# A hybrid mixer block on one core: gates, branch outputs and merge token-major with 512-column moving weights, paired scan heads, new lane paces

## The chip, the cores and the metric

The kernel runs on one core of one Trainium2 chip. The time is device microseconds of one execution. The kernel before takes 2150.59 us, the median of three runs (2144.82 to 2153.54). One more execution was profiled; its own time is 2151.65 us and its span, from the first instruction to the last, is 2149.9 us.

## The reference, cut to what matters

One layer on 256 tokens of width 2048, with a second sequence of 256 context tokens that only feeds the scans' start states. All data is float32.

```python
h  = rms_norm(x, norm_g[0]) * (1 + sc1) + sh1           # sc, sh, g come from c @ mod_w
u  = h @ w_in                                           # 2048 -> 14168 columns, the last 8192 are gates
u_ssd, u_rwkv, u_conv, u_fft, u_gate = split(u)
p_ssd  = ssd_branch(u_ssd)     @ ssd_out                # chunked scan, 12 heads of 64, 4 groups
p_rwkv = rwkv_branch(u_rwkv)   @ rwkv_out               # 8 heads of 64, forward and backward
p_conv = conformer_branch(u_conv) @ conv_out            # 31-tap depthwise convolution
p_fft  = fourier_branch(u_fft) @ fourier_out
gates  = sigmoid(u_gate).reshape(b, l, 4, 2048)
m = gates[:,:,0]*p_conv + gates[:,:,1]*p_ssd + gates[:,:,2]*p_fft + gates[:,:,3]*p_rwkv
y = m @ w_o
x = x + g1 * rms_norm(y, norm_g[1])
h = rms_norm(x, norm_g[2]) * (1 + sc2) + sh2
out = x + g2 * rms_norm(square(relu(h @ mlp_up)) @ mlp_down, norm_g[3])
```

In the scan, each head of 128-token chunks is `(C B^T * L) xd` inside the chunk plus `C state * exp(a)`; the two directions are summed, multiplied by `silu(z)` and normed over all 768 channels before `ssd_out`. The context is scanned for its states alone.

## The kernel before, in words

Each large product is done with three float32r products: a weight and an activation are both split into a rounded part `hi` and a rest `lo`, and hi·hi, hi·lo and lo·hi are summed in PSUM (`mm3`, lines 178 to 180). A **unit** is two k-tiles of 128 rows by 512 weight columns, 512 KB. SyncE fetches it into `raw` (line 155, three buffers), ScalarE rounds it to `hi` (line 166), VectorE subtracts to get `lo` (line 167), five buffers of 512 columns each. `block` makes a product feature-major: the weight is the stationary operand of a matmul, 128 columns at a time, and 256 tokens are streamed past it, 24 matmuls of 256 columns for a unit. `rowblock` makes it token-major: 128 tokens of the activation are stationary and 512 weight columns are streamed, 12 matmuls of 512 columns. Before the change `rowblock` serves the Fourier input, `w_o` and `mlp_down`; `block` serves everything else.

The order of the work: start-up (norms, modulation, first input columns, to about 200 us), the other input columns, 16 **gate blocks** of 8 units each (`mid2`, 640 to 1206 us), the four **branch outputs** (`outs`, in the order rwkv, fft, conv, ssd; 36 units, to about 1300 us), `w_o`, and the two halves of the MLP (from 1405 us to the end). A gate block goes through tanh into a buffer `gs` and to DRAM (`g_d`), and `outs` reads it back as `gt`, computes `(gt + 1) * acc` on VectorE and adds it to the merged `m`; `m` is split into the stationary tiles `hx` of `w_o`.

Beside this **foreground** run **lanes**: generators for the RWKV scan, the 31 taps, the chunked scan (`ssd`, line 1256 on), Fourier and conformer, and a lane that multiplies `mod_w` on VectorE (`rm` loads, line 1448; `macc`, line 1455). After every unit `step` gives each lane a budget of 2.4 times its rate, and the lane issues code until that is used up; a lane's instructions carry a priority offset (`ROFF`, `SOFF`, `COFF`, `TOFF`) by which the scheduler may put them ahead of earlier foreground code. The scheduler fixes the order on each engine when the program is built; every engine then works through its list strictly in that order. A branch output whose lane isn't done first drains that lane (`while n not in self.f_done: self.step(4.0)`).

The chunked scan starts when the RWKV scan has passed a point in its last quarter: `side_setup` loads constants, then for each of 4 groups a 5-tap convolution (`conv5`, lines 1247 to 1253), `C B^T` (1344), states (1364), and for each of 3 heads a table of decays (GpSimd 1374, ScalarE 1378 to 1388), two products (VectorE 1389 to 1399) and four matmuls (1407, 1409) of 64 output rows into half of a PSUM bank. Each second head closes a pair (VectorE 1416, 1419). When all six pairs are there, `chnorm` norms them (1220 to 1232) and they are split for `ssd_out`.

Of the kernel before, what the change touches and what calls it, by code (L numbers as in the profile page):

```python
# [9 lines left out]
ALU = mybir.AluOpType  # L10
P = 128
OFFS = 100
RATE_RWKV = 1.4
RATE_SIDE = .508
RATE_CONV = .279
AHEAD = 2
S2 = 11
ROFF = 100
SOFF = 100
S1 = 14  # L20
WT = dict(a=1.0, A=.813, b=.999, c=.72)
MR = .26, .26, .109, .244
HB = 5
B4 = 8
COFF = -100
MB = 3
XB = 8
MW = 6
RATE_TAPS = .183
TOFF = -200  # L30
GR = 1, 1, 2, 2, 2, 4, 4
RAWB = 3
# [61 lines left out]
class K:  # L94
# [493 lines left out]
    def mid2(self, prep, er, open_ssd, open_side):  # L588
# [18 lines left out]
        cols(C_VAL, self.evac_val)  # L607
        self.lane(self.taps(), rate=RATE_TAPS, offs=TOFF)
# [3 lines left out]
        cols(C_Z + 512, lambda i, ps: self.spill(self.cz_d[4], ps), 2)  # L612
        ssd = side = False
        for b in range(16):
            cols(C_G + 512 * b, gate(b))
            if not ssd and {("A", 3), ("b", 3), ("c", 2)} <= self.rw_done:

                ssd = True
                for st in prep:
                    st.close()  # L620
                self.sd = open_ssd()
                self.side_setup()
                self.lane(self.ssd(), rate=RATE_SIDE, offs=SOFF)
            if not side and not self.rwl["gens"]:
                side = True
                er.close()
                self.fc = open_side()
                self.lane(self.fft(), self.conv(), rate=RATE_CONV, offs=COFF)
# [627 lines left out]
    def ssd(self):  # L1256
# [66 lines left out]
        py = None  # L1323
        for hf in range(2):
            xtk = self.S("b6", [P, 4, 384])
            for f in range(3):
# [9 lines left out]
            for gl in range(2):  # L1336
# [30 lines left out]
                for hl in range(3):  # L1367
# [28 lines left out]
                    for d in range(2):  # L1396
# [2 lines left out]
                        nc.vector.scalar_tensor_tensor(Ce[:, d, l2], row[:, 1 - d, d], et[:, 2 + d, hd[d]:hd[d] + 1],  # L1399
                                                       Cc[:, l2], op0=ALU.mult, op1=ALU.mult)  # L1400
                    yield 2.5
                    if h % 2 == 0:
# [106 lines left out]
    def outs(self, op):  # L1509
# [3 lines left out]
        for n in ("rwkv", "fft", "conv", "ssd"):  # L1513
# [12 lines left out]
                F = [(F[0][:, i], F[1][:, i]) for i in range(k)]  # L1526
            for b in range(4):
                gt = [self.t(op, "gt", [P, 512], bufs=4) for _ in range(2)]
                for i in range(2):
                    nc.sync.dma_start(gt[i], self.g_d[(gi * 16 + b * 4) // 2 + i])  # L1530
                acc = [self.t(self.pa, "acc", [P, 512]) for _ in range(2)]
                for u in range(k // 2):
                    wu = self.unit([(self.wap(io[wname][0], 2 * u, 2, 512 * b, 512), 0)], 2, 512)
                    for f in range(4):
                        for i in range(2):
# [12 lines left out]
                for i in range(2):  # L1548
                    m, om = half(self.m[b], i), half(old, i)
                    if first:  # L1550
                        nc.vector.scalar_tensor_tensor(m, gt[i], 1.0, acc[i], op0=ALU.add, op1=ALU.mult)
                    else:
                        nc.vector.scalar_tensor_tensor(gt[i], gt[i], 1.0, acc[i], op0=ALU.add, op1=ALU.mult)
                        (nc.vector if n == "ssd" else nc.gpsimd).tensor_tensor(m, om, gt[i], op=ALU.add)
# [188 lines left out]
```

## Time and profile before

| | |
|---|---|
| median of three runs | 2150.59 us |
| profiled execution, its own time | 2151.65 us |
| its span | 2149.9 us |
| TensorE matmuls busy | 2058.0 us, 96% |
| VectorE busy | 1503.0 us, 70% |
| ScalarE busy | 1022.7 us, 48% |
| GpSimd busy | 251.9 us, 12% |
| mean granted TensorE clock | 0.990 |

How to read it: matmuls overlap one another, so an interval between two starts, not a duration, is what a matmul costs; a stretch that is 100% busy divided by its count gives that. The profile counts an instruction in the stretch it touches. A float32 matmul without the hand-made split is recorded twice.

### The profile page before, as it was taken

Reading aid. Unit: us, or ns where it says so; the run is one execution under the profiler, and the core shown is the slowest. Engines: PE = TensorE matmul, PEld = TensorE weight load, DVE = VectorE, ACT = ScalarE, POOL = GpSimd, SP = SyncE. Lnnn points to the kernel's source line nnn. Section 1 sums busy time; section 2 is a strip of 40 time slices with the busy share of each in tenths; the row PEclk is TensorE's granted clock in tenths of the full one; section 3 lists DMA queues with packets and bytes.
Section 4 is the critical chain, followed back from the end, with each engine's and each line's share of the span. In section 5 each row is a group of like instructions: output and inputs, shape, how many; then the busy total and the mean of one; then the engine's idle time right before and its main releaser. Section 6 shows DMA issues by size and latency. Waiting matters only on the chain.

```text
span 2149.9 us, 39741 instructions
## 1 busy us (share of the span) xinstructions
PE 2058.0 (96%) x14894; PEld 1884.8 (88%) x14894; DVE 1503.0 (70%) x2699; ACT 1022.7 (48%) x1934; POOL 251.9 (12%) x285
## 2 busy tenths in 40 slices
PE   6999999999999999899999999999999999999997
PEld 5758999998989999798888998899998889999886
DVE  5645875679999779587987787565766655555555
ACT  4212443454654554355666645464554444545443
POOL 1001430022131022021221140000000000000001
PEclk9999999999999999899999999999999999999999
DMA  9983636767666765579876677546867666666554
GB/s 337 318 273 106 186 87 203 234 165 219 197 187 201 214 185 167 177 219 299 265 247 197 205 270 263 188 124 184 262 205 271 234 210 185 185 185 192 192 194 157
DMA packets 310828, 450.99 MB, mean 210 GB/s; under 512 B 70969, under 2 KB 116700, under 8 KB 310124
## 3 DMA queue, kind: packets, MB, share of 16 engines
q1 hardware_dynamic: 308716, 441.86, 65.9%
q10 hardware_dynamic: 1472, 6.49, 0.9%
q8 instruction: 117, 1.92, 0.4%
q14 instruction: 75, 0.61, 0.1%
q0 software_dynamic: 448, 0.11, 0.0%
HBM read 424.22 MB, written 24.16 MB: 209 GB/s over the span
## 4 chain that ended last, share of the span: by engine, by line
PE 71%; DVE 11%; DMA 10%; issue 3%; SPq 2%; ACT 1%; POOL 1%; DVEq 0%; ACTq 0%; POOLq 0%
PE acc L180 20%; PE acc L179 20%; PE acc L178 20%; DMA rm<-in_mod_w 3%; DVE lo L167 2%; DMA raw<-in_w_in 2%; PE sm L282 2%; DVE macc L1455 2%; PE sm L1009 1%; DMA t<-scrA 1%; ACT hi L166 1%; DMA scrA<-x 1%; DMA raw<-in_fourier_out 1%; DVE tm L800 1%; SPq L278 1%
## 5 line engine op out<-in xcount | busy, mean ns | idle before, releaser
L167 DVE TENSOR_TENSOR lo<-raw,hi 128x512 fp32r<-128x512 f32 x1096 | 760.8, 712 | 434.4 <-ACT hi L166 414.6
L166 ACT CAST hi<-raw 128x512 fp32r<-128x512 f32 x1096 | 651.6, 617 | 800.0 <-PE acc L179 442.6
L180 PE MATMUL acc<-h,lo 128*128 128x256 f32 x3056 | 861.6, 286 | 16.1 <-DVE lo L167 15.8
L178 PE MATMUL acc<-h,hi 128*128 128x256 f32 x3056 | 865.7, 286 | 7.7 <-ACT hi L166 5.0
L179 PE MATMUL acc<-h,hi 128*128 128x256 f32 x3056 | 864.7, 285 | 1.5 <-DVE h L173 1.5
L180 PEld LDWEIGHTS acc<-h,lo 128*128 128x128 f32 x3056 | 575.2, 190 | 31.0 <-DVE lo L167 21.4
L178 PEld LDWEIGHTS acc<-h,hi 128*128 128x128 f32 x3056 | 578.4, 190 | 27.0 <-issue 11.8
L179 PEld LDWEIGHTS acc<-h,hi 128*128 128x128 f32 x3056 | 580.0, 190 | 16.4 <-issue 13.4
L1455 DVE SCALAR_TENSOR_TENSOR macc<-rm,sct,macc 128x512 f32<-128x512 f32 x240 | 193.1, 805 | 68.4 <-DMA rm<-in_mod_w 66.9
L179 PE MATMUL acc<-lo,uh 128*128 128x512 f32 x512 | 200.1, 391 | 0.0
L180 PE MATMUL acc<-hi,ul 128*128 128x512 f32 x512 | 199.3, 389 | 0.0
L178 PE MATMUL acc<-hi,uh 128*128 128x512 f32 x512 | 179.0, 389 | 0.0
L178 PEld LDWEIGHTS acc<-hi,uh 128*128 128x128 f32 x512 | 96.1, 188 | 19.9
L179 PEld LDWEIGHTS acc<-lo,uh 128*128 128x128 f32 x512 | 96.1, 188 | 19.9 <-DVE lo L167 0.2
L180 PEld LDWEIGHTS acc<-hi,ul 128*128 128x128 f32 x512 | 96.1, 188 | 19.8
L1689 POOL TENSOR_TENSOR yg<-yg,grow 128x512 f32<-128x512 f32 x8 | 10.9, 1368 | 721.5 <-ACT junk L1688 721.5
L179 PE MATMUL acc<-lo,h 128*128 128x512 f32 x160 | 63.9, 399 | 1.6 <-DVE lo L167 1.6
L180 PE MATMUL acc<-hi,h 128*128 128x512 f32 x160 | 63.3, 396 | 0.0
L1180 DVE SCALAR_TENSOR_TENSOR cv<-vp,col,cv 128x256 f32<-128x256 f32 x120 | 62.7, 523 | 0.4
L472 DVE TENSOR_TENSOR ua<-acc,ua 128x512 f32<-128x512 f32 (+1 forms) x50 | 34.0, 687 | 38.9 <-PE acc L180 38.6
L178 PE MATMUL acc<-hi,h 128*128 128x512 f32 x160 | 57.5, 396 | 1.1 <-ACT hi L166 1.1
L282 PE MATMUL sm<-mw,s 128*32 128x256 f32 (+2 forms) x448 | 57.0, 450 | 0.0
(379 smaller groups left out, 2476.7 us busy)
## 6 DMA issues: line engine op xcount, KB each, us to landing
raw<-in_w_in SPq DMA_DIRECT2D x216, 512.0 KB, 4.5
rm<-in_mod_w SPq DMA_DIRECT2D x256, 256.0 KB, 3.6
raw<-in_mlp_up SPq DMA_DIRECT2D x128, 512.0 KB, 3.6
raw<-in_mlp_down SPq DMA_DIRECT2D x128, 512.0 KB, 4.0
mw<-in_mod_w SPq DMA_DIRECT2D x64, 512.0 KB, 6.1
raw<-in_w_o SPq DMA_DIRECT2D x32, 512.0 KB, 3.6
gd<-gs SPq DMA_DIRECT2D x32, 256.0 KB, 4.3
gt<-gd SPq DMA_DIRECT2D x32, 256.0 KB, 3.4
```

Source lines behind the costliest of these rows:

```text
L166: nc.scalar.copy(b, a)
L167: nc.vector.tensor_tensor(c, a, b.bitcast(F32), op=ALU.subtract)
L178: nc.tensor.matmul(out, w[0], x[0], start=st, stop=False, skip_group_check=True)
L179: nc.tensor.matmul(out, w[0], x[1], start=False, stop=False, skip_group_check=True)
L180: nc.tensor.matmul(out, w[1], x[0], start=False, stop=sp, skip_group_check=True)
L278: nc.sync.dma_start(raw, self.wap(self.io["mod_w"][0], k, ke, c0, w))
L282: nc.tensor.matmul(ps[32 * j:32 * j + 32, :], self.s32[:, u + i, :], ws[i], start=u + i < 4, stop=u + i >= KT - 4, skip_group_check=True)
L472: nc.vector.tensor_tensor(ua[:m], ps[:m], ua[:m], op=ALU.add)
L800: nc.vector.tensor_tensor(o, Y[:, :r, u:u + 1].broadcast_to([P, r, n]), U[:, u:u + 1, u + 1:].broadcast_to([P, r, n]), op=ALU.mult)
L1009: nc.tensor.matmul(ch(ps, i), self.tb[n][d][:, i], ch(v, i), start=True, stop=True)
L1180: nc.vector.scalar_tensor_tensor(o, v, w, o, op0=ALU.mult, op1=ALU.add)
L1455: nc.vector.scalar_tensor_tensor(acc, raw, w, acc, op0=ALU.mult, op1=ALU.add)
```

## The change

- A gate block now goes through `rowblock`: the normed activation is stationary, 512 gate columns are streamed. The gates are stored token-major, 128 tokens by 512 columns to a tile, in as many tiles as before.
- The branch outputs go through `rowblock` in the same way, and `m` is kept token-major. Since `w_o` needs the features on the partitions, the new `mcols` transposes `m` with 32 matmuls against the identity, two PSUM banks for each 512 columns, and splits from PSUM. For 512 columns it is called one block later, for the last at the end.
- The even head of a scan pair issues no matmuls of its own; the odd head issues all eight, alternating between the halves of the bank.
- Rates, priority offsets and weights of the lanes have other values, and the RWKV lane has one buffer of tag `x2` fewer.

```diff
-RATE_RWKV = 1.4
-RATE_SIDE = .508
+RATE_RWKV = 1.451
+RATE_SIDE = 0.69
...
-SOFF = 100
+SOFF = 30
...
-RATE_TAPS = .183
+RATE_TAPS = 0.348
...
         def gate(b):
-            def evac(i, ps):
+
+            def evac(t, acc):
                 o = self.GS()
-                nc.scalar.activation(o, ps, AF.Tanh, scale=0.5)
-                nc.sync.dma_start(self.g_d[2 * b + i], o)
-            return evac
+                nc.scalar.activation(o, acc, AF.Tanh, scale=0.5)
+                nc.sync.dma_start(self.g_d[2 * b + t], o)
+            self.rowblock(win, C_G + 512 * b, range(KT), lambda kt: self.h("x", kt), evac)
...
+                    terms = [(xtk[:, 2 + i, xo:xo + 64], G[:, i]) for i in range(2)]
+                    terms += [(S0[:, d, 64 * hl:64 * hl + 64], Ce[:, d]) for d in range(2)]
                     if h % 2 == 0:
+                        even = terms
+                    else:
                         py = self.psm()
-                    o = py[64 * (h % 2):64 * (h % 2) + 64, :TOK]
-                    xo = (192 * gl + 64 * hl)
-                    for i in range(2):
-                        nc.tensor.matmul(o, xtk[:, 2 + i, xo:xo + 64], G[:, i], start=i == 0, stop=False)
-                    for d in range(2):
-                        nc.tensor.matmul(o, S0[:, d, 64 * hl:64 * hl + 64], Ce[:, d], start=False, stop=d == 1)
+                        for n in range(4):
+                            for j, (w, v) in enumerate((even[n], terms[n])):
+                                nc.tensor.matmul(py[64 * j:64 * j + 64, :TOK], w, v, start=n == 0, stop=n == 3,
+                                                 skip_group_check=True)
...
-                acc = [self.t(self.pa, "acc", [P, 512]) for _ in range(2)]
-                for u in range(k // 2):
-                    wu = self.unit([(self.wap(io[wname][0], 2 * u, 2, 512 * b, 512), 0)], 2, 512)
-                    for f in range(4):
-                        for i in range(2):
-                            kt = 2 * u + i
-                            c = (f % 2) * TOK
-                            self.mm3(acc[f // 2][:, c:c + TOK], (wu[i][0][:, f * P:f * P + P], wu[i][1][:, f * P:f * P + P]),
-                                     F[kt], u == 0 and i == 0 and f % 2 == 0,
-                                     u == k // 2 - 1 and i == 1)
-                    self.step(2.4)
...
+                self.rowblock(io[wname][0], 512 * b, range(k), lambda kt: F[kt], evac)
+                if n == "ssd":
+                    if b == 0:
+                        self.hx = ([], [])
+                    else:
+                        self.mcols(b - 1)
             first = False
-        self.hx = ([], [])
-        for b in range(4):
-            self.hsplit(self.hx, self.m[b], self.p0)
+        self.mcols(3)
+
+    def mcols(self, b):
+
+        nc = self.nc
+        m = self.m[b].rearrange("p f t -> p (f t)").rearrange("p (t c) -> p t c", t=2)
+        for i in range(0, 4, 2):
+            ps = self.psm()
+            for q in range(2):
+                for t in range(2):
+                    o = q * TOK + t * P
+                    nc.tensor.transpose(ps[:, o:o + P], m[:, t, (i + q) * P:(i + q) * P + P], self.cs("ident"))
+            self.hsplit(self.hx, ps.rearrange("p (q c) -> p q c", q=2), self.p0, i)
```

The order of instructions moves far beyond these lines, since the lanes are issued at other places. Three places follow. The line numbers of the changed kernel differ by a few; each sentence names the lines.

**TensorE, the end of the chunked scan.** Before, its last pair of heads (1407, 1409 into `sm_14824`) stands among the matmuls of the first branch output (`acc_14754`, `acc_14755`), with two more branch outputs still to come ahead of `ssd_out`:

```order
L178 MATMUL acc_14755<-f_2872_14746,hi_14796 128x256
L179 MATMUL acc_14755<-f_2873_14747,hi_14796 128x256
L1407 MATMUL sm_14824<-s_2902_14884,b_2585_13090 64x256 x2
L1409 MATMUL sm_14824<-s_2904_14893,s_2825_14487 64x256 x2
L180 MATMUL acc_14754<-f_2872_14746,lo_14797 128x256
L178 MATMUL acc_14754<-f_2872_14746,hi_14792 128x256
L179 MATMUL acc_14754<-f_2873_14747,hi_14792 128x256
L180 MATMUL acc_14754<-f_2872_14746,lo_14793 128x256
```

Now the last group's `C B^T` (1345), states (1365) and its pairs (1413) stand behind the last matmul of the third branch output (`acc_13914`), and no foreground matmul follows until the norm is done:

```order
L179 MATMUL acc_13914<-lo_13944,f_3019_13743 128x512
L180 MATMUL acc_13914<-hi_13943,f_3020_13744 128x512
L1345 MATMUL sm_12304<-s_2629_12189,s_2628_12188 128x256 x2
L1351 MATMUL sm_12309<-cst,s_2628_12188 128x128 x2
L1365 MATMUL sm_12315<-s_2660_12316,s_2657_12312 128x192 x2
L1413 MATMUL sm_12423<-s_2611_12122,b_2469_11522 64x256
L1365 MATMUL sm_12315<-s_2661_12320,s_2657_12312 128x192 x2
L1413 MATMUL sm_12423<-s_2670_12359,b_2469_11522 64x256
L1413 MATMUL sm_12423<-s_2611_12122,b_2469_11522 64x256
L1413 MATMUL sm_12423<-s_2670_12359,b_2469_11522 64x256
L1413 MATMUL sm_12423<-s_2613_12131,s_2563_11918 64x256
```

In the changed program 26 rows, 30 matmuls of the scan and its norm, stand in one piece here, and then the first matmul of `ssd_out`, whose stationary operand is the scan's result.

**VectorE, the same place.** Before, the two evacuations of a third-branch block (1553) have splits (167) for the last branch behind them:

```order
L1553 SCALAR_TENSOR_TENSOR gt_15709<-gt_15709,acc_15713 128x512
L1553 SCALAR_TENSOR_TENSOR gt_15710<-gt_15710,acc_15714 128x512
L167 TENSOR_TENSOR lo_15834<-raw_15827,hi_15833 128x512
L167 TENSOR_TENSOR lo_15864<-raw_15861,hi_15863 128x512
L167 TENSOR_TENSOR lo_15868<-raw_15861,hi_15867 128x512
L167 TENSOR_TENSOR lo_15908<-raw_15905,hi_15907 128x512
L167 TENSOR_TENSOR lo_15912<-raw_15905,hi_15911 128x512
L167 TENSOR_TENSOR lo_15942<-raw_15939,hi_15941 128x512
```

Now the evacuation of the third branch's last accumulator (1548, `acc_13914`) stands ahead of the last tap of the last group's convolution (1250), and the rest of the scan, 29 rows to the split of its result, stands behind that, ahead of the next `lo` but one:

```order
L167 TENSOR_TENSOR lo_13998<-raw_13991,hi_13997 128x512
L1548 SCALAR_TENSOR_TENSOR gt_13910<-gt_13910,acc_13914 128x512
L1250 SCALAR_TENSOR_TENSOR s_2628_12188<-pd_12190,col_9690,s_2628_12188 128x512
L167 TENSOR_TENSOR lo_14016<-raw_14013,hi_14015 128x512
L1254 TENSOR_TENSOR s_2628_12188<-s_2628_12188,s_2641_12243 128x512
L1254 TENSOR_TENSOR s_2629_12189<-s_2629_12189,s_2648_12278 128x256
L1360 TENSOR_TENSOR s_2660_12316<-b_2469_11522,s_wg 128x384
L1360 TENSOR_TENSOR s_2661_12320<-b_2469_11522,s_wg 128x384
L1391 SCALAR_TENSOR_TENSOR s_2670_12359<-s_2669_12351,s_dt,s_2655_12307 128x128 x2
L1400 SCALAR_TENSOR_TENSOR s_2672_12368<-s_2667_12347,s_et,s_2629_12189 128x128 x2
```

The scan's last group has moved from among the foreground to behind it.

**SyncE's queue, the set-up of the chunked scan.** Before, between two `raw` loads there stand 54 transfers, 14 of them `rm` loads of the modulation lane; a piece of that:

```order
L1109 DMA cst_10470<-in_cst 128x512
L239 DMA pk_10472<-in_ssd_conv_w 70x128
L1448 DMA rm_10462<-in_mod_w 128x512
L1001 DMA tb_2817<-scrD_2812 32x4x32 x2
L1001 DMA tb_2814<-scrD_2812 32x4x32 x2
L239 DMA pk_10472<-in_ssd_conv_b 14x128
L239 DMA pk_10472<-in_ssd_norm_g 6x128
L239 DMA pk_10472<-in_conv_ln_g 4x128
L239 DMA pk_10472<-in_conv_ln_b 4x128
L1448 DMA rm_10573<-in_mod_w 128x512
L1448 DMA rm_10647<-in_mod_w 128x512
L1001 DMA tb_2816<-scrA_2810 32x4x32 x2
```

Now the 54 have become one gap of 14 transfers and one of 19 with two `raw` loads between them, and no `rm` load stands in either; the end of the second:

```order
L239 DMA pk_9682<-in_ssd_conv_b 14x128
L239 DMA pk_9682<-in_ssd_norm_g 6x128
L239 DMA pk_9682<-in_conv_ln_g 4x128
L239 DMA pk_9682<-in_conv_ln_b 4x128
L1002 DMA tb_2815<-scrA_2810 32x4x32 x2
L1242 DMA pd_10267<-ssdd_2361 128x2x256
L1242 DMA pd_10096<-ssdd_2360 128x2x256
L1242 DMA pd_10341<-ssdd_2362 128x2x256
L605 DMA gd_2390<-gs_11246 128x512
L155 DMA raw_11450<-in_w_in 128x2x512
L155 DMA raw_11500<-in_w_in 128x2x512
```

The `rm` loads have moved to later gate blocks, a few between each two `raw` loads.

## Rows read from the trace of the kernel before

**Rows 1.** page of before, part 1: engine, busy us, share, instructions.

```profile
PE 2058.0 (96%) x14894; PEld 1884.8 (88%) x14894; DVE 1503.0 (70%) x2699; ACT 1022.7 (48%) x1934; POOL 251.9 (12%) x285
```

**Rows 2.** busy time of each engine by stretch; the first line names columns.

```profile
core 0: us, PE busy (x) PEld busy (x) DVE busy (x) ACT busy (x) POOL busy (x), PEclk, DMA share, GB/s
500.00:700.00 200.00, 192.09 (x1529) 183.01 (x1530) 195.53 (x422) 106.19 (x210) 36.90 (x28) 1.00 0.69 202
860.00:910.00 50.00, 41.14 (x293) 38.91 (x293) 25.20 (x47) 15.75 (x33) 0.37 (x6) 0.83 0.61 181
900.00:1210.00 310.00, 295.96 (x2255) 274.12 (x2256) 254.09 (x455) 181.19 (x382) 67.48 (x95) 1.00 0.75 237
```

**Rows 3.** the same view, in three stretches without a lane of matmuls.

```profile
1430.00:1590.00 160.00, 160.00 (x1355) 160.00 (x1354) 100.33 (x157) 79.78 (x140) 0.00 (x0) 1.00 0.70 211
1330.00:1400.00 70.00, 70.00 (x302) 56.32 (x301) 39.14 (x59) 35.19 (x64) 0.00 (x0) 1.00 0.60 196
2000.00:2050.00 50.00, 50.00 (x222) 41.39 (x221) 28.59 (x39) 23.87 (x41) 2.64 (x2) 1.00 0.57 191
```

**Rows 4.** TensorE in order of time, one scan head: start, us, line, tiles.

```profile
1204.46 1.08 PE L1407 MATMUL sm<-s,b 128*64 128x256 f32 x4
1205.38 1.03 PE L1409 MATMUL sm<-s,s 128*64 128x256 f32 x4
```

**Rows 5.** the same view in the start-up, four-column-group matmuls.

```profile
59.68 1.26 PE L282 MATMUL sm<-mw,s 128*32 128x256 f32 x20
```

**Rows 6.** the same view, a run of 128-wide matmuls.

```profile
1404.63 7.31 PE L1616 MATMUL sm<-cst 128*128 128x128 f32 x64
```

**Rows 7.** SyncE's DMA queue in order of time, when the scan is set up.

```profile
850.19 1.80 SPq L155 DMA_DIRECT2D raw<-in_w_in  x2
869.97 2.31 SPq L1448 DMA_DIRECT2D rm<-in_mod_w  x2
892.66 0.43 SPq L155 DMA_DIRECT2D raw<-in_w_in  x1
```

**Rows 8.** view of Rows 2, five of these microseconds.

```profile
885.00:890.00 5.00, 4.04 (x16) 3.56 (x16) 2.59 (x4) 1.38 (x3) 0.00 (x0) 0.50 0.87 234
```

**Rows 9.** VectorE by line and shape, 640 to 1300 us: busy, mean ns.

```profile
L167 DVE TENSOR_TENSOR lo<-raw,hi 128x512 fp32r<-128x512 f32 x315 | 226.6, 738 | 58.9 <-ACT hi L166 56.5 <-PE acc L180 1.8
L1249 DVE SCALAR_TENSOR_TENSOR s<-pd,col,s 128x512 f32<-128x512 f32 x40 | 32.6, 815 | 0.4 <-ACT s L1247 0.3
L1390 DVE SCALAR_TENSOR_TENSOR s<-s,s_dt,s 128x128 f32<-128x128 f32 x24 | 13.3, 586 | 2.0 <-ACT s L1380 1.9
L1553 DVE SCALAR_TENSOR_TENSOR gt<-gt,acc 128x512 f32<-128x512 f32 x20 | 12.9, 678 | 0.0
L1253 DVE TENSOR_TENSOR s<-s,s 128x512 f32<-128x512 f32 x10 | 7.4, 743 | 2.9 <-POOL s L658 2.9
L1232 DVE SCALAR_TENSOR_TENSOR b<-b,col,s 128x256 f32<-128x256 f32 x6 | 2.5, 478 | 0.0
L1226 DVE RECIPROCAL s<-s 128x256 f32<-128x256 f32 x1 | 1.8, 1753 | 1.1 <-ACT s L1225 1.1
```

**Rows 10.** ScalarE, the same view, 900 to 1300 us.

```profile
L1378 ACT ACTIVATE s<-s,s_nb 128x128 f32<-128x128 f32 x48 | 15.4, 392 | 6.7 <-POOL s L1374 6.6
L657 ACT ACTIVATE s<-s 128x512 f32<-128x512 f32 x10 | 6.3, 630 | 1.7 <-DVE s L1249 1.7
L1225 ACT ACT_TABLE_LOAD x2 | 2.6, 1283 | 0.0
```

**Rows 11.** GpSimd, the same view, 900 to 1300 us.

```profile
L1554 POOL TENSOR_TENSOR h<-h,gt 128x512 f32<-128x512 f32 x16 | 24.0, 1524 | 50.0 <-DVE gt L1553 50.0
L1374 POOL TENSOR_TENSOR s<-s,cst 128x512 f32<-128x512 f32 x12 | 18.3, 1526 | 94.7 <-DVE macc L1455 39.3 <-PE acc L180 33.0 <-DMA s<-crow 22.3
L1398 POOL TENSOR_TENSOR s<-s,s 128x128 f32<-128x128 f32 x24 | 14.1, 609 | 21.5 <-ACT s L1381 21.5
L658 POOL TENSOR_SCALAR s<-s 128x512 f32<-128x512 f32 x10 | 10.2, 1017 | 27.9 <-ACT s L657 27.9
```

More of the change, by code (lines that the diff above doesn't have):

```diff
@@ L12 @@
 OFFS = 100
-RATE_RWKV = 1.4
-RATE_SIDE = .508
-RATE_CONV = .279
+RATE_RWKV = 1.451
+RATE_SIDE = 0.69
+RATE_CONV = 0.28
 AHEAD = 2
 S2 = 11
-ROFF = 100
-SOFF = 100
+ROFF = 68
+SOFF = 30
 S1 = 14
-WT = dict(a=1.0, A=.813, b=.999, c=.72)
-MR = .26, .26, .109, .244
+WT = {'a': 1.0, 'A': 0.728, 'b': 1.021, 'c': 0.887}
+MR = (0.26, 0.264, 0.109, 0.244)
 HB = 5
 B4 = 8
-COFF = -100
+COFF = -295
 MB = 3
-XB = 8
+XB = 7
 MW = 6
-RATE_TAPS = .183
+RATE_TAPS = 0.348
 TOFF = -200
@@ L614, in mid2 @@
         for b in range(16):
-            cols(C_G + 512 * b, gate(b))
+            gate(b)
             if not ssd and {("A", 3), ("b", 3), ("c", 2)} <= self.rw_done:
@@ L1322, in ssd @@
         neg = self.cst2[:, 256:512].rearrange("p (o d l) -> p o d l", o=1, d=2).broadcast_to([P, 2, 2, P])
-        py = None
+        py = even = None
         for hf in range(2):
@@ L1401, in ssd @@
                     yield 2.5
+                    xo = (192 * gl + 64 * hl)
+                    terms = [(xtk[:, 2 + i, xo:xo + 64], G[:, i]) for i in range(2)]
+                    terms += [(S0[:, d, 64 * hl:64 * hl + 64], Ce[:, d]) for d in range(2)]
                     if h % 2 == 0:
+                        even = terms
+                    else:
                         py = self.psm()
-                    o = py[64 * (h % 2):64 * (h % 2) + 64, :TOK]
-                    xo = (192 * gl + 64 * hl)
-                    for i in range(2):
-                        nc.tensor.matmul(o, xtk[:, 2 + i, xo:xo + 64], G[:, i], start=i == 0, stop=False)
-                    for d in range(2):
-                        nc.tensor.matmul(o, S0[:, d, 64 * hl:64 * hl + 64], Ce[:, d], start=False, stop=d == 1)
+                        for n in range(4):
+                            for j, (w, v) in enumerate((even[n], terms[n])):
+                                nc.tensor.matmul(py[64 * j:64 * j + 64, :TOK], w, v, start=n == 0, stop=n == 3,
+                                                 skip_group_check=True)
                     yield 0.5
@@ L1528, in outs @@
                 gt = [self.t(op, "gt", [P, 512], bufs=4) for _ in range(2)]
-                for i in range(2):
-                    nc.sync.dma_start(gt[i], self.g_d[(gi * 16 + b * 4) // 2 + i])
-                acc = [self.t(self.pa, "acc", [P, 512]) for _ in range(2)]
-                for u in range(k // 2):
-                    wu = self.unit([(self.wap(io[wname][0], 2 * u, 2, 512 * b, 512), 0)], 2, 512)
-                    for f in range(4):
-                        for i in range(2):
-                            kt = 2 * u + i
-                            c = (f % 2) * TOK
-                            self.mm3(acc[f // 2][:, c:c + TOK], (wu[i][0][:, f * P:f * P + P], wu[i][1][:, f * P:f * P + P]),
-                                     F[kt], u == 0 and i == 0 and f % 2 == 0,
-                                     u == k // 2 - 1 and i == 1)
-                    self.step(2.4)
+                for t in range(2):
+                    nc.sync.dma_start(gt[t], self.g_d[2 * (4 * gi + b) + t])
                 if first:
@@ L1547, in outs, with evac @@
                     self.m[b] = self.t(op, "m", [P, 4, TOK])
-                for i in range(2):
-                    m, om = half(self.m[b], i), half(old, i)
+                def evac(t, acc):
+                    m, om = half(self.m[b], t), half(old, t)
                     if first:
-                        nc.vector.scalar_tensor_tensor(m, gt[i], 1.0, acc[i], op0=ALU.add, op1=ALU.mult)
+                        nc.vector.scalar_tensor_tensor(m, gt[t], 1.0, acc, op0=ALU.add, op1=ALU.mult)
                     else:
-                        nc.vector.scalar_tensor_tensor(gt[i], gt[i], 1.0, acc[i], op0=ALU.add, op1=ALU.mult)
-                        (nc.vector if n == "ssd" else nc.gpsimd).tensor_tensor(m, om, gt[i], op=ALU.add)
-            first = False
-        self.hx = ([], [])
-        for b in range(4):
-            self.hsplit(self.hx, self.m[b], self.p0)
+                        nc.vector.scalar_tensor_tensor(gt[t], gt[t], 1.0, acc, op0=ALU.add, op1=ALU.mult)
+                        (nc.vector if n == "ssd" else nc.gpsimd).tensor_tensor(m, om, gt[t], op=ALU.add)
+                self.rowblock(io[wname][0], 512 * b, range(k), lambda kt: F[kt], evac)
[4 more added lines that the diff above has]
+                        self.mcols(b - 1)
+            first = False
+        self.mcols(3)
[5 more added lines that the diff above has]
+            for q in range(2):
+                for t in range(2):
+                    o = q * TOK + t * P
+                    nc.tensor.transpose(ps[:, o:o + P], m[:, t, (i + q) * P:(i + q) * P + P], self.cs("ident"))
+            self.hsplit(self.hx, ps.rearrange("p (q c) -> p q c", q=2), self.p0, i)
     def tail(self):
```

## The prediction

> **What bounds the kernel now.** I read the page's busy times first, then the stretches, then the lines of the stretch that the change touches. TensorE is busy 96% of the span and VectorE 70% [rows 1]: the reader is to see that a microsecond taken off TensorE's list is a microsecond gained wherever nothing else is late, and that the next engine isn't far. The stretches split this up. In the MLP and `w_o` TensorE has no idle time at all [rows 3], and nothing of the change lies there but the start of `w_o`. Between 500 and 700 us VectorE is busy 195.5 of 200 us and TensorE 192.1; over the gates with the chunked scan, 900 to 1210 us, they have 254.1 and 296.0 of 310 [rows 2]. So the stretch that is changed is bound by TensorE, with some 5% of stalls in it where a lane, a load or VectorE is late. One place is worse: from 860 to 910 us TensorE is idle 8.9 us and its granted clock averages 0.83 [rows 2]; in the middle of that the clock stands at 0.50, the lower of its two levels, 1.2 GHz [rows 8]. SyncE's queue shows why: between the `raw` loads at 850 and at 892.66 us there is none, only set-up transfers of the scan and `rm` loads that each wait for VectorE [rows 7].
>
> I make the sum against the profiled execution, 2151.65 us; the median of the runs is 1.06 us less.
>
> **A. Gates and branches.** 16 gate blocks of 8 units and 36 units of the branches are 164 units. A unit was 24 matmuls of 256 columns; a stretch full of these has 1355 in 160 us, 118.1 ns each, 2.834 us a unit [rows 3]. It becomes 12 matmuls of 512 columns. `w_o` has 302 in 70 us, 231.8 ns, 2.782 us a unit; `mlp_down` has 222 in 50 us, 225.2 ns, 2.703 us [rows 3]. So 0.052 or 0.131 us a unit, 8.6 or 21.5 us in all. `w_o` has the gates' stationary tiles, but `mlp_down` runs through the same function; I take the middle, -15. The same tanh, the same stores and loads of the gates and the same evacuations remain.
>
> **A rule on the same thing.** In the Trainium skill, "TensorE: Matmul & The Clock Gate", section "Back-to-back issue gap", a stream costs its columns at 2.4 GHz and 2.5 ns a matmul: 262 cycles for 256 columns, 518 for 512. By that, as an estimate from the page, a unit falls from 2.62 to 2.59 us and the 164 units give 5 us and not 15. The trace's 256-column matmuls are 9 ns slower than this and its 512-column ones 9 to 16 ns, so the rule is below both, and what is disputed is how much of that is paid for each matmul.
>
> **B. Pairs of heads.** The 48 matmuls of the heads are 96 recorded passes; one head's eight start at 1204.46 and the last ends at 1206.41, and L1409's first start is 0.92 us after L1407's, so a pass costs about 0.23 us [rows 4] and all cost some 21 us. Alternating halves can at best run two at once. The start-up has matmuls on quarters of the columns: 20 of them in 1.26 us, 63 ns each, with the same 256 columns [rows 5]. So the halves do overlap in this chip's traces: 10.4 us at best, 0 at worst. Two of six pairs fall into the stretch of E and are counted there: -7.
>
> **C. Transposes.** `mcols` adds 32 matmuls of 128 columns. 64 passes of that width take 7.31 us [rows 6], 0.114 each: +3.6, or up to +7.3 if a transpose makes two passes. Its splits are as many columns as before, on engines that have room there. In the order of TensorE the first units of `w_o` stand ahead of the last transposes, so their latency is covered; without that cover it would be a `gt` evacuation, an add and a split, some 2 us.
>
> **D. The set-up of the scan.** The gap of 54 transfers with 14 `rm` loads becomes gaps of 14 and of 19 without any. What it cost: 8.9 us idle, and of the clock 17% of 50 us, that is 17 us at half rate, of which TensorE worked some 10 and lost 5: 14 us. Of the new gaps the longer is 19 times about 0.45 us of the queue (an `rm` pair takes 2.31 us with its waits, a lone load 0.43 [rows 7]), 8.6 us, and three loaded buffers cover three units, 8.4 us. The scratch of the solve must land in the shorter one before its readers. I take -12, with 0 and -14 as ends.
>
> **E. The end of the scan is no longer covered.** This is the step that the diff doesn't show and the order does. On VectorE, the evacuation of the last accumulator of the third branch now stands ahead of the last group's last tap, the silu, three heads, the norm and the splits, and TensorE's next matmul of `ssd_out` needs these. VectorE's evacuation waits for TensorE's last matmul of that branch; so from there TensorE has nothing but the scan's own matmuls until a serial chain is through. Its links, by [rows 9 to 11]: evacuation 0.68 and tap 0.82; then ScalarE's tanh 0.63 and GpSimd's half-plus 1.02, which queues behind two adds of 1.52 for the evacuated gates, so about 4.1 us after the start; silu 0.74 and a smaller one, `C B^T`, its copies and the states, 3.3 more: 8.1. Then the heads, which go round GpSimd and ScalarE: table add 1.53, four exps of 0.39 and one of four times the width, as wide as the tanh, 0.63, 2.2, two products of 0.61, 1.22, 4.95 a head. The first head's add is early, so 0.79 for two exps more and 2.2; then 1.22, 1.7 of GpSimd for the closed pair, and the second's 1.53 and 2.2; 1.22, 1.53 and 2.2 for the third; 0.79 of ScalarE and 1.2 of VectorE behind it: 16.6, so 24.7. Then eight passes' worth of matmuls and their drain, 1.9, two VectorE steps, 1.0, a square and a last sum beside a table load of 1.28, a root of 0.48, the reciprocal 1.75, six steps of 0.48, and the first split, 0.42: 9.7. Together 34 us. In that time TensorE does what it must do anyway, about 8.5 us (`C B^T` 0.9, states 1.3, the two pairs' passes 3.5, sums 2.6, transposes 0.2). [...] So 34 - 8.5 + 2.5 = +28. The ends: VectorE's own 29 rows and the evacuation, tap and split ahead of them are some 24 us, less 8.5, +15; with the clock at half for all of the scan's matmuls, +36. Before, the last pair stood in the first branch with two branches of cover, and this cost nothing.
>
> **A second rule, against B.** The Trainium skill, same page, section "The mechanism" (packing small matmuls), lets a weight load overlap matmuls in flight only where the row group differs; two halves of the columns have the same rows. By it B would be 0 and the sum 7 us higher. But [rows 5] has weights in the same rows too, at 63 ns a matmul, so the trace doesn't bear it out.
>
> **F. Other paces.** Two effects I cannot tell apart in size. The `rm` loads and their `macc` steps move out of the stretch of the RWKV scan, where 500 to 700 us lacks 7.9 us of TensorE [rows 2]; perhaps -5. Against that, the chunked scan starts later and is pressed into fewer, shorter units: from its first tap to the third branch's end VectorE now has 172 splits to 200 before, but as many of the scan's taps; the sum of durations (splits at 0.74, the 512-column taps at 0.82, the rest likewise [rows 9]) falls from 334 to 310 us, while the units' time falls from 283 to 239. VectorE was busy 82% there already [rows 2]; perhaps +5. I take 0, with 12 each way.
>
> Sum: -15 - 7 + 3.6 - 12 + 28 + 0 = -2.4; 2149.3 by the profiled execution, 2148 by the median.
>
> **The rivals.**
> *The bubble is short and the stream pays in full.* A at `mlp_down`'s rate -21.5, B -7, C +3.6, D -14, E at +20, F -7 as the stalls of 500 to 700 us go: -26, 2125 us. For it: TensorE is the bound nearly everywhere and every unit gains; against it: E is a chain of single steps, each with its row, and it would have to lose a quarter.
> *The scan starves the last gate blocks.* From the scan's first tap to the third branch's end VectorE's list has 310 us of durations for 86 units, 3.60 us a unit (before 334 for 100, 3.34), and TensorE's has 239 us of units and some 45 of the lanes' matmuls, 3.30 a unit (before 283 and 55, 3.38). Before, TensorE's share was the longer; now VectorE's is. Where it decides, the stretch is 86 times 0.30, 26 us longer than the sum has it: 2174 us. The point is a unit whose share of VectorE is over TensorE's. For it: 254.1 of 310 us busy with the lighter load; against it: durations on VectorE overlap a little, and it was busy 98% from 500 to 700 us with TensorE still at 96% [rows 2].
> *The wide stream doesn't pay.* If the 6144 columns of a unit set its pace, in 12 matmuls as in 24, A is nothing and the time 2163 us. For it: 256 columns at 118.1 ns are within 2% of half of `w_o`'s 512; against it: `mlp_down`'s rate [rows 3]. By the page's rule above, A would be 5 us and this case's time 2158 us.
>
> **How the numbers follow.** Less than 0.5%, 10.8 us, can't be told from no change here. The forecast, 0.40, has its own range from 2136 to 2160: faster 0.05, same 0.33, slower 0.02. The short bubble, 0.30: faster 0.29, same 0.01. The starved gates, 0.20: slower 0.19, same 0.01. The stream that doesn't pay, 0.10: same 0.05, slower 0.05. Together faster 0.34, same 0.40, slower 0.26. The range: all of A, D, E and F at their low ends is 36 us less, 2114; the high end is the starved gates, 2176.
>
> **What would show it.** Right: in the changed profile gate units of 12 matmuls at 225 to 232 ns; between the last matmul of the third branch and the first of `ssd_out` a stretch of 30 to 38 us in which TensorE has the scan alone, at a lowered clock; the passes of a pair at half the pitch; no hole at the scan's set-up. Wrong: no such stretch, or one under 20 us (E); a hole of over 8 us at the set-up (D); TensorE waiting for `lo` in the last gate blocks for over 15 us more than before (the second rival).

## The result and the profile after

The changed kernel takes 2163.13 us (median of 6 runs, 2158.95 to 2165.31), the kernel before 2145.78 in runs beside it (2141.35 to 2153.54). The ratio is 1.0068, 95% interval 1.0047 to 1.009: slower by 0.68%, some 15 us, where the prediction had 2 us less. The profiled execution's span is 2163.5 us.

The page of the changed kernel, its busy times [rows 1]:

```profile
PE 2053.5 (95%) x12958; PEld 1781.9 (82%) x12958; DVE 1508.9 (70%) x2703; ACT 1025.0 (47%) x1938; POOL 242.9 (11%) x285
```

TensorE has 1936 matmuls fewer and is busy 4.5 us less in a span 13.6 us longer: the loss is waiting and a lower clock, not more work. The busy times by stretch in the changed kernel (columns as in [rows 2]) say where:

```profile
860.00:910.00 50.00, 48.49 (x285) 41.40 (x285) 35.47 (x74) 27.33 (x56) 6.09 (x11) 1.00 0.57 168
860.00:950.00 90.00, 82.35 (x459) 69.39 (x459) 62.70 (x127) 48.51 (x96) 8.36 (x20) 0.96 0.63 191
950.00:1243.60 293.60, 279.35 (x1286) 219.09 (x1284) 253.99 (x426) 160.62 (x325) 70.74 (x85) 0.98 0.80 261
1200.00:1243.60 43.60, 37.01 (x141) 26.64 (x139) 43.60 (x63) 23.27 (x52) 25.31 (x22) 0.88 0.74 233
1243.60:1288.00 44.40, 19.64 (x59) 10.71 (x58) 23.79 (x42) 16.43 (x44) 14.30 (x18) 0.62 0.27 84
```

The same in the kernel before (the first stretch is in [rows 2], and the last row takes two in one):

```profile
860.00:950.00 90.00, 81.14 (x631) 78.71 (x631) 61.90 (x121) 37.17 (x73) 10.89 (x20) 0.91 0.62 186
950.00:1243.60 293.60, 279.15 (x2092) 256.71 (x2091) 235.08 (x403) 171.99 (x363) 59.72 (x82) 1.00 0.76 243
1200.00:1288.00 88.00, 87.32 (x696) 84.31 (x695) 73.89 (x106) 42.85 (x83) 28.02 (x21) 1.00 0.74 247
```

From 860 to 910 us TensorE has gained 7 us and the full clock. The hole at the scan's set-up is not gone, though: it has moved with the set-up and shrunk, to a gap of 5.3 us at 917 us. Over 860 to 950 us, which holds the set-up in both kernels, TensorE is busy only 1.2 us more than before, at a mean clock of 0.96 against 0.91. SyncE's queue around the set-up in the changed kernel, with the 19 other transfers between these two rows:

```profile
896.70 0.91 SPq L155 DMA_DIRECT2D raw<-in_w_in  x2
...
915.61 1.50 SPq L155 DMA_DIRECT2D raw<-in_w_in  x3
```

From 1243.6 to 1288 us it has 59 matmuls in 44.4 us, at a mean granted clock of 0.62: the scan's uncovered end. In the 43.6 us ahead, which the prediction did not single out, VectorE is busy all the time and the clock is already at 0.88: there the end of the second branch and the third wait for VectorE. Before, TensorE was full in both. But waiting of this kind is not new, it has moved with the scan: from 950 to 1243.6 us, which holds most of the scan in either kernel, TensorE is busy 279.35 us now and 279.15 before. Only the clock is a little lower, 0.98 against 1.00. What TensorE waited for from 1195 to 1300 us, in the changed kernel:

```profile
PE sm L1413 <- DVE s L1395: 10.1, 2, 6.6
PE sm L1345 <- DVE s L1254: 9.2, 1, 9.2
PE acc L179 <- DVE lo L167: 6.4, 4, 3.2
PE acc L178 <- ACT s L172: 3.9, 1, 3.9
```

And TensorE in order of time, at the end of the third branch (start, us, line, tiles, idle before):

```profile
1239.14 0.39 PE L179 MATMUL acc<-lo,f 128*128 128x512 f32 x1
...
1243.22 0.39 PE L180 MATMUL acc<-hi,f 128*128 128x512 f32 x1
1252.81 2.04 PE L1345 MATMUL sm<-s,s 128*128 128x256 f32 x4 [9.20 <-DVE s L1254]
...
1266.69 1.54 PE L1413 MATMUL sm<-s,b 128*64 128x256 f32 x5 [6.61 <-DVE s L1395]
...
1273.87 1.08 PE L1413 MATMUL sm<-s,b 128*64 128x256 f32 x2 [3.51 <-DVE s L1395]
...
1288.13 0.51 PE L178 MATMUL acc<-hi,s 128*128 128x512 f32 x1 [3.89 <-ACT s L172]
```

The gaps are the chain that term E lists: silu, `C B^T` (L1345), the heads (L1413), the split ahead of `ssd_out`. One link is not in that list. SyncE's queue in these microseconds:

```profile
SPq L1372 <- PE sm L1413: 9.9, 1, 9.9
```

L1372 loads a head's table row. Its buffer comes free when an earlier head's matmuls have read theirs, so the heads don't overlap as the sum had them.

The changed matmuls themselves, in a run of gate units and in one pair of heads:

```profile
937.47 0.40 PE L178 MATMUL acc<-hi,h 128*128 128x512 f32 x1
...
941.91 0.39 PE L178 MATMUL acc<-hi,h 128*128 128x512 f32 x1
...
1066.33 0.86 PE L1413 MATMUL sm<-s,b 128*64 128x256 f32 x5
1066.82 0.38 PE L1413 MATMUL sm<-s,s 128*64 128x256 f32 x1
1067.03 0.38 PE L1413 MATMUL sm<-s,b 128*64 128x256 f32 x1
1067.03 1.24 PE L1413 MATMUL sm<-s,s 128*64 128x256 f32 x7
```

Between the first two starts lie 19 intervals, 0.234 us each; the branch rows above have 18 in 4.08 us, 0.227. A pair's passes of the two halves run side by side: 1.94 us for two heads, where one took 1.95 [rows 4].

### The profile page after: what moved, and what is told of

It is laid out like the page before. It is cut to its first block, busy times and chain, and to the rows that moved or that the text cites. A ratio compares the mean times of both kernels' runs of the same rounds, so it can differ in the third digit from the quotient of the medians.

```text
span 2163.5 us, 35759 instructions
## 1 busy us (share of the span) xinstructions
PE 2053.5 (95%) x12958; PEld 1781.9 (82%) x12958; DVE 1508.9 (70%) x2703; ACT 1025.0 (47%) x1938; POOL 242.9 (11%) x285
## 4 chain that ended last, share of the span: by engine, by line
PE 70%; DVE 14%; DMA 8%; issue 4%; ACT 1%; SPq 1%; POOL 1%; DVEq 0%; POOLq 0%; ACTq 0%
PE acc L179 20%; PE acc L178 20%; PE acc L180 20%; DVE lo L167 3%; DMA rm<-in_mod_w 2%; PE sm L282 2%; DVE cv L1181 2%; DMA raw<-in_w_in 2%; DVE macc L1460 2%; PE sm L1010 1%; DVE t L803 1%; DVE tm L801 1%; DMA vp<-vpd 1%; DMA s<-crow 1%; SPq L278 1%
## 5 line engine op out<-in xcount | busy, mean ns | idle before, releaser
L180 PE MATMUL acc<-h,lo 128*128 128x256 f32 x2032 | 574.8, 284 | 6.2 <-DVE lo L167 6.2
L178 PE MATMUL acc<-h,hi 128*128 128x256 f32 x2032 | 574.7, 285 | 2.6 <-ACT h L172 2.6
L179 PE MATMUL acc<-h,hi 128*128 128x256 f32 x2032 | 575.0, 284 | 1.3 <-DVE h L173 1.3
L178 PEld LDWEIGHTS acc<-h,hi 128*128 128x128 f32 x2032 | 383.5, 189 | 17.6 <-issue 9.7
L179 PEld LDWEIGHTS acc<-h,hi 128*128 128x128 f32 x2032 | 385.2, 190 | 15.4 <-issue 13.2
L180 PEld LDWEIGHTS acc<-h,lo 128*128 128x128 f32 x2032 | 383.8, 189 | 14.0 <-DVE lo L167 7.6
L179 PE MATMUL acc<-lo,h 128*128 128x512 f32 x672 | 271.2, 405 | 8.7 <-DVE lo L167 8.7
L180 PE MATMUL acc<-hi,h 128*128 128x512 f32 x672 | 266.6, 399 | 0.0
L178 PE MATMUL acc<-hi,h 128*128 128x512 f32 x672 | 255.4, 402 | 7.1 <-ACT hi L166 7.1
L179 PEld LDWEIGHTS acc<-lo,h 128*128 128x128 f32 x672 | 126.7, 189 | 42.9 <-DVE lo L167 14.8
L178 PEld LDWEIGHTS acc<-hi,h 128*128 128x128 f32 x672 | 126.2, 189 | 38.4 <-ACT hi L166 8.4
L180 PEld LDWEIGHTS acc<-hi,h 128*128 128x128 f32 x672 | 126.5, 188 | 28.0 <-issue 0.7
```

Of the source, the lines that this page charges most:

```text
L178: nc.tensor.matmul(out, w[0], x[0], start=st, stop=False, skip_group_check=True)
L179: nc.tensor.matmul(out, w[0], x[1], start=False, stop=False, skip_group_check=True)
L180: nc.tensor.matmul(out, w[1], x[0], start=False, stop=sp, skip_group_check=True)
```

## The experiments

Theory 1: the loss is the uncovered end of the scan and the branches starved ahead of it, and the token-major units bring it. Theory 2: the new paces do. Theory 3: 512-column matmuls and transposes don't pay. Ratios are to the kernel before, timed beside each.

**The change in parts.** Ten constants put back:

```diff
-RATE_SIDE = 0.69
-SOFF = 30
+RATE_SIDE = .508
+SOFF = 100
...
```

> The changed code with the old numbers of the background lanes (ten constants). Theory 1 (the loss is the uncovered end of the scan and the branches that VectorE starves ahead of it, and the token-major units bring it, whatever the paces): the uncovered stretch between the third and the last branch stays, 35 to 55 us with the clock near 0.6, and the time is 2150 to 2175, slower than before or near it. Theory 2 (the new paces put the scan late): the stretch closes and the time falls to 2120 to 2135. Theory 3 (512-column matmuls and the added transposes don't pay): no stretch, and 2145 to 2155.

2177.32 us, 1.0126 (1.0104 to 1.0147), 2 us above the range of theory 1. The same constants put into the kernel before:

> The kernel before with the new numbers of the lanes alone. Theory 1: the scan ends under matmuls of the stream as it did, and the time is within 10 us of before (2136 to 2156). Theory 2: the scan ends late here too, with an uncovered stretch of over 25 us ahead of the last branch, and the time is 2160 to 2185. Theory 3 says nothing of it: as before.

2154.38 us, 1.002 (1.0006 to 1.0034). Only the gates token-major, in the kernel before:

```diff
-            cols(C_G + 512 * b, gate(b))
+            gate(b)
...
+            self.rowblock(win, C_G + 512 * b, range(KT), lambda kt: self.h("x", kt), evac)
```

> The kernel before with only the sixteen gate blocks token-major (the gate values then reach the old merge in another layout, so the merged values are not the reference's; the work is the same). Theory 1: this edit alone brings the uncovered end of the scan (35 to 55 us ahead of the last branch) against some 18 us of gain (9 of shorter matmuls, 9 of the set-up hole): 2160 to 2180. Theory 2: no stretch, 2125 to 2135. Theory 3: no stretch, 2143 to 2155.

2180.62 us, 1.0135 (1.0112 to 1.0159), at the top of theory 1's range. All of the rest but the paces:

> The kernel before with the paired heads, the token-major branches and the transposes, but the old gates and the old paces (the gate values have the old layout, so the merged values are not the reference's; the work is the same). Theory 1: the scan ends covered, and the gain of the pairs (7 to 10) and the branches (2 to 3) less the transposes (4) is seen: 2132 to 2143. Theory 2: the same, since the paces are old. Theory 3: the branches and transposes cost, 2143 to 2155.

2141.79 us, 0.9954 (0.9938 to 0.9969). And the heads alone:

> The kernel before with only the paired heads. Theory 1 and the prediction's term B: 0 to 10 us less than before, at 2136 to 2146, for 48 of 96 head matmuls would begin some 10 ns behind another one. If the alternation costs (two groups open in a bank at once), it is not faster: 2146 to 2155.

2143.43 us, 0.9977 (0.9962 to 0.9992).

Theory 2 falls: the old paces make the changed kernel slower, and the new ones cost the kernel before 4 us. Theory 3 falls: heads, branches and transposes gain 10 us, about 5 of them the heads'. One edit, the gates, costs 29 us by itself. The traces show what it does to the scan. The first and last `C B^T` matmuls and norm sums (minimum, median, maximum ns; first and last start), before:

```profile
L1344 PE MATMUL sm<-s,s x16: 377/379/462, 988.3 to 1177.9; 128*128 128x256 f32 x16
L1221 PE MATMUL sm<-s,cst x12: 377/379/379, 1212.4 to 1216.6; 128*128 128x256 f32 x12
```

in the changed kernel:

```profile
L1345 PE MATMUL sm<-s,s x16: 377/379/764, 1028.3 to 1254.2; 128*128 128x256 f32 x16
L1222 PE MATMUL sm<-s,cst x12: 379/558/796, 1275.6 to 1283.9; 128*128 128x256 f32 x12
```

with the gates alone:

```profile
L1345 PE MATMUL sm<-s,s x16: 378/379/483, 1059.2 to 1269.1; 128*128 128x256 f32 x16
L1222 PE MATMUL sm<-s,cst x12: 379/379/536, 1293.7 to 1299.4; 128*128 128x256 f32 x12
```

and with the new paces alone:

```profile
L1344 PE MATMUL sm<-s,s x16: 377/379/462, 949.8 to 1155.1; 128*128 128x256 f32 x16
```

The scan is not longer by much (240 us with the gates alone, 228 before); it begins 71 us later. The new paces by themselves begin it 38 us earlier.

**The price of the uncovered end.** The scan's fourth group left out, of the changed kernel and of before:

```diff
+                if g == 3:
+                    nc.vector.tensor_copy(yz[:, 4:6], yz[:, 2:4])
+                    yield 1.0
+                    continue
```

> The changed code without the fourth of the scan's four groups (three heads, two convolutions; the outputs of its channel tiles are copied from another, so the output is not the reference's). Theory 1 (the end of the scan stands on the path): the uncovered 44 us ahead of the last branch shrink to under 10, the branches ahead of it run without waits, and the time falls by 35 to 55 below the changed kernel, to 2108 to 2128. Theory 3 (wide matmuls and transposes don't pay, the scan's end is beside the point): it falls by the 24 to 40 narrow matmuls alone, some 10 us, to 2150 to 2155.

2126.42 us, 0.9896 (0.9875 to 0.9917).

> The kernel before with the same group left out, as a control. Theory 1: there the scan ends under the branches' matmuls, so only the group's own TensorE time goes (36 matmuls and transposes, about 10 us) and some VectorE load: 2130 to 2143. If it fell by as much as the changed kernel does, the group's work and not its place would be what costs.

2140.36 us, 0.996 (0.9944 to 0.9976).

The changed kernel falls from 1.0068 to 0.9896, 37 us, the control 9. So the group's place at the end costs 28 us net. With it left out, the changed kernel's stretches:

```profile
1200.00:1244.00 44.00, 34.13 (x146) 24.59 (x144) 44.00 (x64) 25.66 (x59) 25.55 (x22) 1.00 0.75 249
1244.00:1300.00 56.00, 53.28 (x234) 42.47 (x235) 40.13 (x66) 24.51 (x43) 1.93 (x2) 0.94 0.69 225
```

The stretch from 1244 us is covered again; the one ahead of it is still starved, with VectorE busy 44 of 44 us and TensorE idle 9.9. So what came back is the price of the end, and the starved branches, the other half of theory 1, are not shown to add to the loss.

**VectorE in the branches.**

```diff
-(nc.vector if n == "ssd" else nc.gpsimd).tensor_tensor(m, om, gt[t], op=ALU.add)
+nc.vector.tensor_tensor(m, om, gt[t], op=ALU.add)
```

> The changed code with the merge's additions of the second and third branch on VectorE instead of GpSimd. If VectorE's own work is what starves those branches (it was busy all of 1200 to 1243 us), 16 more instructions there make the time 2165 to 2180. If its instructions are only slowed by GpSimd working beside them (those of 0.7 us took up to 2.9), taking the additions off GpSimd gives 5 to 20 us back: 2143 to 2158.

2157.63 us, 1.0037 (1.002 to 1.0053), some 7 us less than the changed kernel (1 to 12 by the two intervals), though VectorE has 16 more instructions. Splits on VectorE from 1195 to 1245 us (busy, mean ns), in the changed kernel and then with the additions moved:

```profile
L167 DVE TENSOR_TENSOR lo<-raw,hi 128x512 fp32r<-128x512 f32 x26 | 24.1, 945 | 0.0
```

```profile
L167 DVE TENSOR_TENSOR lo<-raw,hi 128x512 fp32r<-128x512 f32 x24 | 16.7, 702 | 0.0
```

**Hurrying the scan.** `RATE_SIDE` 1.1, `SOFF` 100, `RATE_CONV` 0.2, `XB` 8 in the changed kernel; then with the additions on VectorE too; then heads and additions in the kernel before:

> The changed code with the scan's lane hurried and the lane of convolution and FFT slowed (RATE_SIDE 1.1, SOFF 100, RATE_CONV 0.2, XB 8): in the order of instructions the last group of the scan then stands under the third branch, ahead of the wait. Theory 1: the uncovered stretch ahead of the last branch shrinks from 44 us to 5 to 25, though VectorE stays full where the branches meet the scan, and the time is 2130 to 2152. Theory 3, or if the pace moves work without shortening the chain: 2155 to 2170.

2162.79 us, 1.0066 (1.0046 to 1.0085): a miss for theory 1, within what was named for a pace that moves work without shortening the chain.

> The same with the merge's additions on VectorE. Theory 1 with what the run of the additions alone gave (7 us): 2125 to 2148, faster than the kernel before. If VectorE is by then what the branches wait for, no faster than without.

2161.58 us, 1.0062 (1.0043 to 1.008): a miss.

> The kernel before with the paired heads and the additions on VectorE: 5 us from the pairs, as measured, and 0 to 5 from the additions, since VectorE is not full in its branches: 2136 to 2145. If VectorE's slow instructions come from GpSimd's work in general, not from these additions, the same as the pairs alone, 2143.

2143.84 us, 0.9979 (0.9963 to 0.9994): no more than the heads give.

The hurried scan gained nothing because the wait only moved. A stretch of it, and the wait on TensorE:

```profile
1150.00:1200.00 50.00, 24.72 (x90) 17.92 (x91) 40.15 (x70) 24.32 (x54) 15.97 (x20) 0.73 0.69 230
```

```profile
PE sm L1413 <- DVE s L1395: 22.3, 4, 18.4
```

A head's matmul now stands ahead of the branches in TensorE's order and waits 18.4 us for VectorE, with the branches' matmuls behind it.

**What delays the scan.** The program of the lanes is the same with the gates alone, so either the 512-column matmuls (theory 1a) or the token-major form whatever its width (1b) puts the scan late. Token-major gates in 256 columns:

```diff
+                for c in range(0, 512, w):
+                    self.mm3(acc[t][:, c:c + w], hs, [x[:, c:c + w] for x in wu[i]],
+                             u == 0 and i == 0 and c == 0, u == n - 1 and i == 1)
...
+            self.rowblock(win, C_G + 512 * b, range(KT), lambda kt: self.h("x", kt), evac, w=TOK)
```

> The changed code with the old paces, and its gates token-major as in the change, but in matmuls of 256 columns (24 a unit, as before) instead of 512 (12). Theory 1a (it is the 512-column gate matmuls that let the stream of gates run ahead of the lanes in the order of instructions): the scan begins within 30 us of where it did before (988 us), ends under the branches, no uncovered stretch, and the time is that of pairs and branches alone, 2136 to 2148. Theory 1b (the token-major form does it, with its accumulators and evacuations in another order, whatever the width): the scan begins near 1055 again and the time is 2165 to 2185, as with the old paces and wide gates.

2137.07 us, 0.9945 (0.9932 to 0.9959).

> The same with the new paces: the changed kernel with nothing but its gate matmuls halved in width. Theory 1a: the scan ends covered, 2132 to 2150, though each gate unit lasts some 0.07 us longer. Theory 1b: as the changed kernel or 9 us above it, 2163 to 2175.

2134.75 us, 0.9939 (0.992 to 0.9957). Then wide gates in some blocks only, `w=512 if b < 3 or b >= 10 else TOK` and `w=512 if b >= 8 else TOK`:

> Old paces, gates of 512 columns in blocks 0 to 2 and 10 to 15, of 256 in blocks 3 to 9, while the scan is opened and fed. Theory 1a: the scan begins within 30 us of before and ends covered, and nine blocks of eight units at 0.07 us give back 5 us more than all narrow: 2130 to 2143. Theory 1b: late scan, 2165 to 2185.

2127.98 us, 0.9908 (0.9889 to 0.9927), 2 us below the range.

> New paces, gates of 512 columns from block 8 on. Theory 1a: the scan ends under the branches but with less to spare (a smaller distance to the last branch in the order of instructions than with all narrow): 2130 to 2152. Theory 1b: 2163 to 2175.

2133.13 us, 0.9924 (0.9908 to 0.994).

Theory 1a stands: from 1.0126 to 0.9945, 38 us, by the width of the gates' matmuls alone, although the narrow ones take longer (0.120 us each, 2.88 us a unit, against 2.81 with 512 columns). The scan with narrow gates and old paces:

```profile
L1345 PE MATMUL sm<-s,s x16: 377/379/463, 989.6 to 1171.8; 128*128 128x256 f32 x16
L1222 PE MATMUL sm<-s,cst x12: 377/378/382, 1200.8 to 1214.0; 128*128 128x256 f32 x12
```

and with the mixed gates the stretch of the branches:

```profile
1200.00:1300.00 100.00, 98.80 (x438) 77.16 (x437) 90.56 (x132) 49.76 (x94) 28.45 (x20) 1.00 0.77 246
```

The scan begins within 10 us of where it did before (978.9 us with the mixed gates), TensorE works 98.8 of 100 us at full clock, and the mixed version is 20 us faster than the kernel before and 34 faster than the change. Its wide gates, in nine blocks that don't put the scan late, gain 8 us over narrow ones throughout.

## Why the prediction was wrong

The bookkeeping first. Take the interval ahead of each of TensorE's matmuls, and its excess over the median for the same form and tiles. Forms and counts alone then give -8 us, the excess from 200 to 1200 us falls by 20, from 1200 to 1300 us it rises by 43, and the rest is -1. That is +14, as measured. The prediction had for the first three -18.4 (A, B, C), -12 (D, with F at 0) and +28 (E). By stretch, the change of the excess is -6 from 860 to 950 us (the set-up), -14 from there to 1100, +3 to 1200, +11 to 1243.6, and +31 from there to the first matmul of `ssd_out`. The three in the middle are waits that moved with the scan; they cancel. (Medians over other groups shift these figures by some us, the first one most.)

**The steps that failed are the sizes of A and D.** They were put at -15 and -12, and are worth 8 and some 6 us of gain. These 13 us are most of the way from -2.4 to +14, and they turn the sign.

*A* was too large. The gates run at 0.234 us a matmul and the branches at 0.227, so 128 units gain 0.030 us and 36 gain 0.114 against the 2.834 of [rows 3]: 8 us, the low end of the range, where the middle was taken. The row to lean on was `w_o`'s, which has the gates' operands. The rule of the Trainium skill that the prediction sets beside A ("TensorE: Matmul & The Clock Gate", section "Back-to-back issue gap") is by that section's own words the gap of an isolated matmul; for 512 columns in a stream it has some 131 ns, which these runs, at 225 to 234, don't bear out.

*B* is right in its mechanism: the passes of a pair take half the time. All six pairs are worth 5 us (2 to 8), where 10.4 was the best case and 7 was put in for four.

*C* was not run apart; with the branches it gives the 5 us between the heads alone and heads with branches, and as those two intervals overlap, even these are not clear of nothing.

*D* was right in kind, but the hole was to vanish and it only shrank and moved. The longer gap between `raw` loads lasted 18.0 us, from 897.6 to 915.6 us, where 8.6 were reckoned for its 19 transfers and three units cover 8.4; before it was 40.7 [rows 7]. Nor do the `rm` loads each wait for VectorE in the kernel before, as the prediction reads them: from 845 to 905 us these waits are five, 3.2 us in all.

*E* is right in place and kind, and near in size: leaving the last group out gave back 28 us net, and the intervals have 31. Its stretch is 44 us and not 34: `C B^T` began 9.6 us after the branch's last matmul, where the links give about 5; the clock was at 0.62 on the mean; and the wait for the row buffer was not in the sum. No run shows the 2.5 us that the sum adds for the clock; what they show is that mean of 0.62 over the stretch.

*F*, the other paces at 0, came out near right by luck, since neither of its two effects is what the runs show. It gives the later scan to the paces, but by themselves they start the scan earlier; they cost the kernel before 4 us and are worth 12 us to the changed one (1.0126 without, 1.0068 with). What starts the scan late is the wide gates. And the starving that F and the second rival feared is no cost on top: what was lost to it from 950 to 1100 us is now lost from 1100 to 1243.6.

Of the rivals, the scan that starves the last gate blocks has its sign, but in the branches behind the gates, 1200 to 1243.6 us, and not its 26 us, for TensorE is busy as long from 950 to 1243.6 us as before. The stream that doesn't pay has the measured time, 2163 us, by luck: A gained half of what was taken, not nothing, and the rest lies in D and E. The short bubble is out by the 44 us.

Behind this lies that A and E were added up as if they were two things. In a program whose instruction order is worked out over all lanes, a unit of 12 instructions in place of 24 changes also where the lanes' instructions stand. With the same program of the lanes, the scan moved by 71 us, and back with the width: A's 8 us are bought with E's 28 to 31. By which of its rules the ordering does this stays open.

## What to carry to other kernels

Before a foreground stream is made cheaper, find the lane that has least to spare behind it, and price how much of that lane's end loses its cover; set that against the gain of the stream. Where instruction order comes from a scheduler, compare the start of each lane in the two traces, not just the edited lines: here half the change was sound and one width, in seven of sixteen blocks, spoiled it. And compare what a stretch holds, not its place on the time axis: a hole or a wait that is gone from 860 us can stand at 917. A wait that is moved forward in an in-order queue is not a wait removed: hurrying the scan put 18 us in the middle for what it took off the end.

## What the hardware showed

VectorE instructions are longer when GpSimd works beside them. In the changed kernel, on VectorE and then on GpSimd:

```profile
1222.63 2.90 DVE L167 TENSOR_TENSOR lo<-raw,hi 128x512 fp32r<-128x512 f32 x2
1225.98 2.90 DVE L167 TENSOR_TENSOR lo<-raw,hi 128x512 fp32r<-128x512 f32 x2
```

```profile
1221.99 2.99 POOL L1549 TENSOR_TENSOR h<-h,gt 128x512 f32<-128x512 f32 x2 [2.08 <-DVE gt L1548]
1224.95 0.84 POOL L659 TENSOR_SCALAR s<-s 128x256 f32<-128x256 f32 x1
1225.76 1.44 POOL L1375 TENSOR_TENSOR s<-s,cst 128x512 f32<-128x512 f32 x1
1227.16 1.18 POOL L1423 TENSOR_TENSOR s<-s,s 128x256 f32<-128x256 f32 x1
```

Splits that take 0.74 us on the mean [rows 9] take 2.90 for two (not for one, as the expectation of the run with the additions moved has it). The Trainium skill, "Advanced Engine Details and Errata", section "GPSIMD Details", says that GpSimd shares a read and a write interface with VectorE and conflicts there with VectorE instructions that have two SBUF inputs, as a split has in `raw` and `hi`. The trace agrees, and 945 against 702 ns is what it was worth here. Moving the additions gave 7 us in the changed kernel, where VectorE is full, and nothing in the kernel with the heads alone. That the 7 us are the shorter splits' alone is not shown: from 1195 to 1300 us SyncE's waits ahead of the loads of `gt` fell as well, from 13.4 to 8.6 us.

The gates' 512-column matmuls follow each other in 0.234 us and the branches' in 0.227, by the same function and at the same clock. Why they differ was not tried.
